# Softmax sums turned on TensorE, evacuating copies given to ScalarE, and 64-column level products, in a four-mixer kernel on one core

## The chip, the cores and the metric

The kernel runs on one core of a Trainium2 chip. The metric is the device time of one execution, in microseconds. A product of two 128-row tiles runs on TensorE (PE), which loads a stationary operand ("weights", the records of PEld) and streams the moving operand past it; VectorE (DVE), ScalarE (ACT) and GpSimd (POOL) do the element-wise work, and every DMA of this kernel is issued by SyncE (SP), in order.

## The reference

x is 1024 tokens by 1024 features in float32. Four mixers follow each other, with normalisations between them:

```python
x = layer_norm(ALPHA * x + gla_mixer(x), ...)        # 4 heads, gated linear attention, chunks of 64
x = layer_norm(ALPHA * x + dilated_mixer(x, k, v))   # 3 groups of windows, 8 query heads, 2 kv heads
for i in (0, 1):
    shift, scale, gate = split(silu(c) @ ada_w[i] + ada_b[i])
    h = rmsnorm(x, g[i]) * (1 + scale) + shift
    x = x + gate * (diff_attention(h) if i == 0 else mla(h))
return rmsnorm(x, final_g)
```

Three places of it matter here. In the gated linear attention, `att[i, j] = sum_d q[i, d] k[j, d] exp(b[i, d] - b[j, d])` for j <= i, with b the running sum of the log gates. In the differential attention each head has two score sets:

```python
p = softmax(sc, axis=-1)
o = (p[:, :, 0] - lam * p[:, :, 1]) @ v          # per head
o = rmsnorm(o, subln_g) * (1 - lambda_init)      # over the head's 128 features
y = (o * silu(z)) @ w_out
```

And the MLA mixer first makes two low-rank projections, normalises them and multiplies them up to heads.

## The kernel before

**Products.** A float32 product is split into three products of fp32r halves (`mm3`, L165 to L167): high by high, high by low, low by high. Weights come by DMA as `wraw` (128x1024) or `wvraw` (128x512), ACT casts them to `whi` or `wvhi` (L192, L204), and `lo` (L150) subtracts to get the low half, on DVE or POOL.

**The order of the work.** PE runs in the order in which the program is written (a manual schedule for PE alone); the other engines' orders, SP's too, are set by the Tile scheduler. Projections are cut into filler units. A `Unit` has a prep (loads and casts) and pieces of some 430 to 655 ns each, and `Fill.give(ns)` puts as many pieces into PE's order as the credit pays for, wherever the main work would leave PE waiting. All filler units, and some of the main work, take their PSUM tile from one pool, "mm", which has two buffers: a piece that begins a third tile waits until the first one has been copied out by its `evac`.

**The stages,** by the profiled execution: gated linear attention to about 395 us (`gla_core`), a boundary (gating, output projection, layer norm) to 520, the preparation of the window attention (gates, V) to 610, its main loop to 1200, a boundary to 1340, the preparation of the differential attention (V, ada) to 1450, its main loop to 2008, a boundary to 2150, the preparation of MLA to 2300, its main loop to 2690, and the final boundary and norm.

**GLA levels** (L465 to L492). Per head, seven levels m = 64, 32, ..., 1. At each one the 1024 positions are pairs of halves of m; `e` holds the decays of earlier halves (L472) and later halves (L473), ACT takes the exponential (L474), DVE multiplies k by it into `ktl` (L476) and q by it in place (L477, 128x1024). Level 64 multiplies `ktl`'s 64 columns by `e`'s 64 (L481). The other six make two PSUM tiles of four 128x128 products each (L489), of which only the later halves' columns are taken by a `copy_predicated` (L490).

**V and gate units.** `u_vs` makes eight units of tokens (st 0 to 7) per group of values; its evac copies 128x256 out of PSUM on ACT for odd st and on DVE for even st (L959 in the window attention, L1285 in the differential attention). `u_gate` (L250) copies a gate's two halves out on ACT (half 0) and DVE (half 1) (L254). MLA's low-rank units copy `lraw` out on DVE (L1485).

**Ada units** (L583 to L589). The prep is eight DVE operations on a 128x4096 weight (one L575, seven L577) that end in `xb`; the piece is one product with `ones` (L583); then DVE masks it, sums it and adds the bias (L586, L588, L589).

**The differential attention's main loop** (L1389 to L1459) runs 66 steps over 8 heads by 8 query tiles. Step i makes the scores of tile i (L1420), their maxima (L1424) and exponentials (L1426), which also give the softmax sums, one column of `dsum` (128x8) for each tile. `combine`, run one step later, joins the two score sets (L1441 to L1443), and after every fourth tile writes four columns of `dsum` to DRAM in token order (L1445):

```python
nc.sync.dma_start(self.dnd[h][:, half(t // 4)].rearrange("o (f p) -> (o p) f", p=128), dsum[:, t - 3:t + 1])
```

Two steps behind the scores, `attend` transposes P (L1240), and copies it out as `PTh` (ACT, L1242) and `PTl` (DVE, L150). After each pair of tiles `pv` multiplies by V (L1365 to L1368), copies the result out as `y` (L1370) and squares it; `norm` sums the squares with a product of ones (L161) and writes them to `d_ms` (L1381). `factors` (L1245) reads the squares (`d_ms`, L1251) and the softmax sums (`d_dn`, L1252) back with tokens on the partitions, works out the reciprocal roots on DVE (L1254 to L1265) and writes them to `d_rs` (L1267). It is called for 14 halves of heads after tile pair (6, 3), for half (7, 0) after (7, 1), and for (7, 1) in the boundary.

Of the kernel before, what the change touches and what calls it, by code (L numbers as in the profile page):

```python
# [11 lines left out]
I32 = mybir.dt.int32  # L12
# [125 lines left out]
class Kern:  # L138
# [124 lines left out]
    def build(self):  # L263
        tc, nc, A = self.tc, self.nc, self.A
        with ExitStack() as ctx:
# [9 lines left out]
            self.ones = cp.tile([128, 128], F32, name="ones")  # L275
            self.ones_r = cp.tile([128, 128], F32R, name="ones_r")
            self.cv = cp.tile([128, 4], F32, name="cv")
# [6 lines left out]
            nc.vector.memset(self.ones_r.bitcast(F32), 1.0)  # L284
# [34 lines left out]
    def gla(self):  # L319
        tc, nc, A = self.tc, self.nc, self.A  # L320
        V, S, G, T = nc.vector, nc.scalar, nc.gpsimd, nc.tensor
        with ExitStack() as ctx:
# [22 lines left out]
            def u_g(h, halves=(0, 1)):  # L345
                return self.u_gate(h, "gla_wg", gp, halves)
# [103 lines left out]
    def gla_core(self, gp, pp, fill, h, qT, kT, v, bs, masks, ahead):  # L450
# [14 lines left out]
        for li, m in enumerate(LEVELS):  # L465
# [11 lines left out]
            V.tensor_tensor(e, qT, e, op=OP.mult)  # L477
            if m == 64:
                pl = pp.tile([128, 8, 64], F32, name="lv")
                for c in range(8):  # L480
                    T.matmul(pl[:64, c, :], kt_[:, c * 128:c * 128 + 64], e[:, c * 128 + 64:c * 128 + 128], start=True, stop=True)  # L481
                V.tensor_copy(att[:64].rearrange("p (c i) -> p c i", i=128)[:, :, 64:128], pl[:64])
                fill.give(2200)
                continue
            for hf in range(2):
                pl = pp.tile([128, 512], F32, name="lv")
                for c in range(4):
                    cc = slice((4 * hf + c) * 128, (4 * hf + c) * 128 + 128)
                    T.matmul(pl[:, c * 128:c * 128 + 128], kt_[:, cc], e[:, cc], start=True, stop=True)  # L489
                V.copy_predicated(view(att[:, half(hf)])[:, :, 1, :],  # L490
                                  masks[:, li * 256:li * 256 + 256].rearrange("p (n m) -> p n m", m=m), view(pl)[:, :, 1, :])
# [189 lines left out]
    def boundary(self, name, wo, res, res_out, warm, ln=None, gate=None, mod=None, normed=False):  # L681
# [151 lines left out]
        for hf, off, n in parts:  # L833
            s = slice(hf * 512 + off, hf * 512 + off + n)
            for kt in range(2 if hf == 0 else 6 if final else 3, 8) if off == 0 else ():
                if normed and hf == 0 and kt == 7:
                    self.factors(bo, [(7, 1)])
# [90 lines left out]
    def swa(self, before):  # L928
# [6 lines left out]
        with ExitStack() as ctx:  # L935
# [13 lines left out]
            with tc.tile_pool(name="swv", bufs=1, reuse_waits="tile") as vp:  # L949
# [235 lines left out]
            def after(h, g):  # L1185
# [13 lines left out]
                if g == 2:  # L1199
                    if h == 2:  # L1200
                        fill.add(u_kk(1, 0))
                    fill.add(self.u_gate(h, "swa_wg", ap, (0, 1) if h > 2 else (1,)))
# [42 lines left out]
    def factors(self, pool, hs):  # L1245

        nc, V = self.nc, self.nc.vector
# [6 lines left out]
        V.scalar_tensor_tensor(e, e, 128.0 * 1e-6, e, op0=OP.mult, op1=OP.mult)  # L1254
        V.tensor_tensor(t, t, e, op=OP.add)
        V.tensor_scalar(t, t, 1.0 / 128.0, None, op0=OP.mult)

        yi = y.bitcast(I32)
        V.tensor_scalar(yi, t.bitcast(I32), 1, None, op0=OP.logical_shift_right)
        V.tensor_scalar(yi, yi, -1.0, float(0x5f3759df), op0=OP.mult, op1=OP.add)  # L1260
        V.tensor_scalar(t, t, -0.5, None, op0=OP.mult)
        for _ in range(4):
            V.tensor_tensor(e, y, y, op=OP.mult)
            V.tensor_tensor(e, e, t, op=OP.mult)
            V.scalar_tensor_tensor(y, e, 1.5, y, op0=OP.add, op1=OP.mult)  # L1265
        for n, (g, hf) in enumerate(hs):
            nc.sync.dma_start(flat(self.rsd[g], hf), y[:, 4 * n:4 * n + 4])  # L1267

    def da(self, before):
# [3 lines left out]
        with ExitStack() as ctx:  # L1273
            with tc.tile_pool(name="dav", bufs=1, reuse_waits="tile") as vp:
# [75 lines left out]
            zs = [self.u_gate(h, "da_wz", dp, (hf,)) for hf, h in [(1, h) for h in range(3)] +  # L1350
# [430 lines left out]
```

## Time and profile before

| | us |
|---|---|
| median of 3 runs | 2798.11 (2795.3 to 2800.18) |
| the profiled execution's own time | 2794.63 |
| its span, first to last instruction | 2792.9 |
| PE busy | 2660.9 (95%) |
| DVE busy | 1890.0 (68%) |
| ACT busy | 1349.2 (48%) |
| POOL busy | 314.6 (11%) |

The profile is of one execution. [...] A wait of PE is idle time of PE with the line of the instruction that waited and the line that ended the wait. The timeline lists single instructions with the idle time before them in brackets. Numbers of lines are those of the kernel before.

### The profile page before, as it was taken

What the parts mean: (1) busy time and instruction counts of PE and PEld (TensorE: products, weight loads), DVE (VectorE), ACT (ScalarE), POOL (GpSimd) and SP (SyncE); (2) the same over time, 40 slices, a digit from 0 to 9 for tenths busy, and PEclk for the clock granted to TensorE, in tenths of its full rate; (3) what the DMA queues carried; (4) which work ended last, traced back from release to release, by engine and by line L of the source; (5) the groups of instructions that cost most, each with busy time, mean ns of one, the idle gap of its engine ahead of it and who ended that gap; (6) DMA issues with size and microseconds to landing.
All of it is one profiled execution on the core that took longest, in us unless ns stands there. A gap on an engine that the chain in (4) does not pass through costs nothing.

```text
span 2792.9 us, 39308 instructions
## 1 busy us (share of the span) xinstructions
PE 2660.9 (95%) x14788; PEld 2234.5 (80%) x14788; DVE 1890.0 (68%) x3478; ACT 1349.2 (48%) x2492; POOL 314.6 (11%) x224
## 2 busy tenths in 40 slices
PE   8999999998999999988999999998799899999998
PEld 7889988887778878776897877786578688888878
DVE  7776547567666666667657788886576627777785
ACT  5444345426344434347515766765445415554563
POOL 0000000000000000000015656664000000000000
PEclk9999999999999999999999999999799999999999
DMA  5310155654111111154642432342275220100143
GB/s 206 107 43 32 49 180 182 210 176 144 50 42 50 46 47 53 50 185 145 228 165 74 63 67 61 66 55 62 90 266 170 68 70 23 33 27 29 39 172 110
DMA packets 163926, 274.70 MB, mean 98 GB/s; under 512 B 32948, under 2 KB 82388, under 8 KB 162072
## 3 DMA queue, kind: packets, MB, share of 16 engines
q1 hardware_dynamic: 163736, 272.19, 31.7%
q8 instruction: 116, 1.90, 0.3%
q14 instruction: 74, 0.61, 0.1%
HBM read 195.48 MB, written 66.17 MB: 94 GB/s over the span
## 4 chain that ended last, share of the span: by engine, by line
PE 67%; DVE 14%; DMA 7%; ACT 7%; issue 3%; SPq 1%; POOL 1%; ACTq 0%; DVEq 0%; POOLq 0%
PE mm L165 14%; PE mm L166 14%; PE mm L167 14%; PE pt L1240 3%; PE sc L1420 3%; PE sc L1657 2%; PE sc L1049 2%; PE lv L489 1%; PE pt L1153 1%; PE sc L166 1%; PE sc L165 1%; PE sc L167 1%; DVE den L1424 1%; PE mm L1623 1%; DVE wlo L150 1%
## 5 line engine op out<-in xcount | busy, mean ns | idle before, releaser
L165 PE MATMUL mm<-xh,whi 128*128 128x512 f32 x1456 | 613.3, 421 | 18.0 <-DVE t L911 6.0
L167 PE MATMUL mm<-xh,wlo 128*128 128x512 f32 x1456 | 574.0, 394 | 2.5 <-POOL wlo L150 1.6
L166 PE MATMUL mm<-xl,whi 128*128 128x512 f32 x1456 | 574.0, 394 | 1.7 <-DVE xl L150 1.7
L165 PEld LDWEIGHTS mm<-xh,whi 128*128 128x128 f32 x1456 | 277.6, 191 | 75.5 <-DVE t L911 7.3
L167 PEld LDWEIGHTS mm<-xh,wlo 128*128 128x128 f32 x1456 | 275.8, 189 | 64.4 <-POOL wlo L150 2.5
L166 PEld LDWEIGHTS mm<-xl,whi 128*128 128x128 f32 x1456 | 277.6, 191 | 52.9 <-DVE xl L150 4.0
L150 POOL TENSOR_TENSOR wlo<-wraw,whi 128x1024 fp32r<-128x1024 f32 x29 | 70.6, 2435 | 1334.9 <-ACT whi L192 1332.9
L165 PE MATMUL mm<-wvhi,xh 128*128 128x256 f32 x704 | 204.6, 291 | 4.8 <-DVE V L959 3.0
L192 ACT CAST whi<-wraw 128x1024 fp32r<-128x1024 f32 (+2 forms) x141 | 135.9, 964 | 138.3 <-PE mm L166 128.9
L167 PE MATMUL mm<-wvhi,xl 128*128 128x256 f32 x704 | 199.2, 283 | 0.1
L166 PE MATMUL mm<-wvlo,xh 128*128 128x256 f32 x704 | 198.6, 282 | 0.0
L1426 ACT ACTIVATE P<-sc,den 128x1024 f32<-128x1024 f32 x128 | 142.9, 1117 | 113.4 <-DVE den L1424 112.8
L1424 DVE TENSOR_REDUCE den<-sc 128x1 f32<-128x1024 f32 x128 | 153.5, 1212 | 3.5 <-PE sc L1420 3.5
L150 DVE TENSOR_TENSOR wlo<-wraw,whi 128x1024 fp32r<-128x1024 f32 (+2 forms) x113 | 123.5, 1093 | 43.8 <-ACT whi L192 40.7
L1043 ACT ACTIVATE P<-P,nm 128x128 f32<-128x128 f32 (+1 forms) x192 | 84.9, 443 | 124.5 <-DVE nm L1041 124.2
L165 PEld LDWEIGHTS mm<-wvhi,xh 128*128 128x128 f32 x704 | 134.0, 190 | 9.9 <-DVE V L959 3.2
L166 PEld LDWEIGHTS mm<-wvlo,xh 128*128 128x128 f32 x704 | 134.5, 191 | 1.3 <-issue 1.0
L167 PEld LDWEIGHTS mm<-wvhi,xl 128*128 128x128 f32 x704 | 133.9, 190 | 0.4 <-DVE xl L150 0.4
L165 PE MATMUL mm<-oh,xh 128*128 128x512 f32 (+1 forms) x336 | 126.1, 375 | 0.3 <-ACT oh L796 0.3
L166 PE MATMUL mm<-ol,xh 128*128 128x512 f32 (+1 forms) x336 | 124.2, 370 | 2.0 <-DVE ol L150 2.0
L167 PE MATMUL mm<-oh,xl 128*128 128x512 f32 (+1 forms) x336 | 123.7, 368 | 0.0
L1053 DVE CUSTOM_DVE_ANT_0 P<-sc,band 128x128 f32<-128x128 f32 (+1 forms) x192 | 59.6, 348 | 71.5 <-PE sc L1049 71.1
(355 smaller groups left out, 6124.5 us busy)
## 6 DMA issues: line engine op xcount, KB each, us to landing
xa<-in_ada_w SPq DMA_DIRECT2D x12, 2048.0 KB
d_z<-zt SPq DMA_DIRECT2D x64, 256.0 KB
oh<-d_z SPq DMA_DIRECT2D x64, 256.0 KB
ol<-d_o SPq DMA_DIRECT2D x64, 256.0 KB
d_r<-X SPq DMA_DIRECT2D x48, 256.0 KB
wraw<-in_swa_wq SPq DMA_DIRECT2D x24, 512.0 KB
res<-d_r SPq DMA_DIRECT2D x40, 256.0 KB
zt<-zt SPq DMA_DIRECT2D x160, 64.0 KB
```

The costliest lines, as they stand in the source:

```text
L150: eng.tensor_tensor(out, src, hi.bitcast(F32), op=OP.subtract)
L165: mm(ps, l[0], r[0], start=first, stop=False)
L166: mm(ps, l[0], r[1], start=False, stop=False)
L167: mm(ps, l[1], r[0], start=False, stop=last)
L192: nc.scalar.copy(hi, raw)
L1043: S.activation(p[:, off:off + w_], p[:, off:off + w_], AF.Exp, bias=nm[:, g, b:b + 1], scale=scale, accum_out=stat(h, g, 1, b))
L1049: T.matmul(sc[:, b % 2, :w_], q[:, b * 128:b * 128 + 128], k[:, k0:k0 + w_], start=True, stop=True)
L1053: V.tensor_tensor_reduce(p[:, off:off + w_], sc[:, b % 2, :w_], mk, 1.0, NEG, op0=OP.add, op1=OP.max, accum_out=stat(h, g, 0, b))
L1240: nc.tensor.transpose(pt[:, i, :], P[:, (4 * j + i) * 128:(4 * j + i) * 128 + 128], self.ident)
L1420: T.matmul(sc[c][:, s], QS[h][c][r, q0:q0 + 128], (KL[h] if k else KH[h][c])[r, s], start=first, stop=not first)
L1424: V.tensor_reduce(dn[:, 2 + c:3 + c], sc[c], AX, OP.max, negate=True)
L1426: S.activation(p, sc[c], AF.Exp, bias=dn[:, 2 + c:3 + c], accum_out=dn[:, 1:2] if c else d0)
```

## The change

It has four parts.

1. **GLA levels.** The query multiplication makes the later halves only: 128x512, into tiles that are named `khT` and `qh` by turns, and no longer in place. The six lower levels' products stream 64 columns in place of 128 (192 products), and a level fills one PSUM tile in place of two. `ones` becomes a view of `ones_r`, which saves one memset.
2. **Softmax sums.** `combine` no longer writes `dsum`. `pv` transposes its four columns on PE (a 4x128 result in unused columns of the PSUM bank that holds its output), ACT copies that out as `dr`, and the write to `d_dn` has 4 rows of 512 bytes. `factors` issues its reads at once, and its DVE work (`rest`) comes two steps later.
3. **Copies.** The copies out of PSUM of the window attention's V, of the differential attention's V, of MLA's `lraw` and of MLA's second gate halves are all made by ACT.
4. **Places of ada units.** In the preparation of the differential attention the first ada product comes three V pieces later and the others at distances of three and four; in MLA's the second one comes after two more gates.

```diff
-    def u_gate(self, h, src, pool, halves=(0, 1), w=None):
+    def u_gate(self, h, src, pool, halves=(0, 1), w=None, act=True):
...
-            (self.nc.vector.tensor_copy if hf else self.nc.scalar.copy)(z, ps)
+            (self.nc.scalar.copy if act or not hf else self.nc.vector.tensor_copy)(z, ps)
...
-            V.tensor_tensor(e, qT, e, op=OP.mult)
+
+            eq = gp.tile([128, 512], F32, name=("khT", "qh")[li % 2])
+            V.tensor_tensor(eq.rearrange("p (n m) -> p n m", m=m), view(qT)[:, :, 1, :], ev[:, :, 1, :], op=OP.mult)
...
+            pl = pp.tile([128, 512], F32, name="lv")
+            for c in range(8):
+                T.matmul(pl[:, c * 64:c * 64 + 64], kt_[:, c * 128:c * 128 + 128], eq[:, c * 64:c * 64 + 64], start=True, stop=True)
             for hf in range(2):
-                pl = pp.tile([128, 512], F32, name="lv")
-                for c in range(4):
-                    cc = slice((4 * hf + c) * 128, (4 * hf + c) * 128 + 128)
-                    T.matmul(pl[:, c * 128:c * 128 + 128], kt_[:, cc], e[:, cc], start=True, stop=True)
...
                 def u_vs(g, sts):
                     def evac(st, ps):
-                        (S.copy if st % 2 else V.tensor_copy)(Vt[g][:, st, :], ps)
+                        S.copy(Vt[g][:, st, :], ps)
...
         for n, (g, hf) in enumerate(hs):
             nc.sync.dma_start(t[:, 4 * n:4 * n + 4], flat(self.msd[g], hf))
             nc.sync.dma_start(e[:, 4 * n:4 * n + 4], flat(self.dnd[g], hf))
-        V.scalar_tensor_tensor(e, e, 128.0 * 1e-6, e, op0=OP.mult, op1=OP.mult)
...
+        def rest():
+            V.scalar_tensor_tensor(e, e, 128.0 * 1e-6, e, op0=OP.mult, op1=OP.mult)
...
+        return rest
...
-                    (S.copy if st % 2 else V.tensor_copy)(t, ps)
+                    S.copy(t, ps)
...
-                    pre.add(u_vs(0, range(4, 8)), u_vs(1, range(4, 5)), ada[0], u_vs(1, range(5, 8)), ada[1], u_vs(2, range(0, 4)), ada[2], u_vs(2, range(4, 8)), ada[3], u_vs(3, range(0, 4)), ada[4], u_vs(3, range(4, 8)), ada[5])
+                    pre.add(u_vs(0, range(4, 8)), u_vs(1, range(4, 8)), ada[0], u_vs(2, range(0, 3)), ada[1], u_vs(2, range(3, 6)), ada[2], u_vs(2, range(6, 8)), u_vs(3, range(0, 1)), ada[3], u_vs(3, range(1, 4)), ada[4], u_vs(3, range(4, 8)), ada[5])
...
-                o = self.mmp.tile([128, 256], F32, name="mm")
+                bank = self.mmp.tile([128, 512], F32, name="mm")
+                o, d = bank[:, :256], bank[0:4, 256:384]
...
+                if due:
+                    T.transpose(d, due[0][2], self.ident)
...
                 nc.sync.dma_start(self.od[h][qb4 // 2][:, s], y)
+                if due:
+                    g, hf, _ = due.pop()
+                    r = dp.tile([128, 128], F32, name="dr")
+                    S.copy(r[0:4], d)
+                    nc.sync.dma_start(self.dnd[g][:, half(hf)].rearrange("o (f p) -> (o f) p", p=128), r[0:4])
...
                 if comb:
                     comb.pop()()
+                if facts and facts[0][0] <= i:
+                    facts.pop()[1]()
...
-                        norm(*nrm)
+                        if f := norm(*nrm):
+                            facts.append((i + 2, f))
...
-                            nc.sync.dma_start(self.dnd[h][:, half(t // 4)].rearrange("o (f p) -> (o p) f", p=128),
-                                              dsum[:, t - 3:t + 1])
+                            due.append((h, t // 4, dsum[:, t - 3:t + 1]))
...
-                        V.tensor_copy(raw[key, hf][:, c, :], ps)
+                        S.copy(raw[key, hf][:, c, :], ps)
...
-                pre.add(self.u_ada(p0, 1, 5, 1), *[self.u_gate(h, "mla_wz", p0) for h in range(3, 8)])
+                late = [self.u_gate(h, "mla_wz", p0) for h in range(3, 8)]
+                pre.add(*late[:2], self.u_ada(p0, 1, 5, 1), *late[2:])
```

The gates of the gated linear attention, of the window attention's main loop and of the differential attention's main loop are called with `act=False` and keep their engines.

How it moves instructions, at three places. **First place:** SP's queue near the end of the differential attention's loop, from the write of the squares of pair (6, 3) to the first reads of half (7, 0). `vr` is `factors`' tile, `d_dn` the softmax sums in DRAM, `d_ms` the squares, `d_rs` the result, `wraw` weights for the boundary. Before:

```order
L179 DMA wraw<-in_w_out 128x1024
L1251 DMA vr<-d_ms 128x4
L1445 DMA d_dn<-dsum 128x4x1
L1371 DMA d_o<-y 128x256
L255 DMA d_z<-zt 128x512
...
L1267 DMA d_rs<-vr 128x4 x14
L1371 DMA d_o<-y 128x256
L1252 DMA vr<-d_dn 128x4
L1381 DMA d_ms<-sq 1x256
L1445 DMA d_dn<-dsum 128x4x1
L1251 DMA vr<-d_ms 128x4
```

With the change:

```order
L1385 DMA d_dn<-dr 4x128
L1254 DMA vr<-d_dn 128x4
L255 DMA d_z<-zt 128x512
L1395 DMA d_ms<-sq 1x256
L179 DMA wraw<-in_w_out 128x1024
L1253 DMA vr<-d_ms 128x4
...
L1271 DMA d_rs<-vr 128x4 x14
L1380 DMA d_o<-y 128x256
L1385 DMA d_dn<-dr 4x128
L1254 DMA vr<-d_dn 128x4
L1395 DMA d_ms<-sq 1x256
L1253 DMA vr<-d_ms 128x4
```

The last read of squares for the 14 halves is no longer followed at once by a write of sums, and the sums of (7, 0) are written after the 14 `d_rs`, directly ahead of their read.

**Second place:** DVE at the same point, around the first instruction of `factors` for the 14 halves (128x56). L1424, with the change L1440, is the maximum of a tile of scores. Before:

```order
L1443 SCALAR_TENSOR_TENSOR P<-P,den 128x1024
L1254 SCALAR_TENSOR_TENSOR vr<-vr 128x56
L150 TENSOR_TENSOR PTl<-pt,PTh 128x4x128
L1424 TENSOR_REDUCE den<-sc 128x1
L150 TENSOR_TENSOR PTl<-pt,PTh 128x4x128
L1424 TENSOR_REDUCE den<-sc 128x1
```

With the change:

```order
L150 TENSOR_TENSOR PTl<-pt,PTh 128x4x128
L1440 TENSOR_REDUCE den<-sc 128x1
L1258 SCALAR_TENSOR_TENSOR vr<-vr 128x56
L1458 RECIPROCAL den<-den 128x1
L1459 SCALAR_TENSOR_TENSOR den<-den,nlam,dsum 128x1
L254 COPY zt<-mm 128x512
L1460 SCALAR_TENSOR_TENSOR P<-P,den 128x1024
```

The first operation of `factors` moves down past six maxima and three combinations (L1443, now L1460). The second one (L1255, now L1259) stays behind the maxima that it followed.

**Third place:** ACT in the preparation of the window attention, where the first four V tiles of the first group are made. L204 casts a piece of V's weights, L741 (now L742) a piece of the normalised x, L959 (now L960) copies a V tile out. Before:

```order
L254 COPY zt<-mm 128x512
L741 CAST xh_70<-X 128x512 x2
L204 CAST wvhi<-wvraw 128x512
L959 COPY V_4095<-mm 128x256
L204 CAST wvhi<-wvraw 128x512
L959 COPY V_4095<-mm 128x256
L755 ACTIVATE rs<-stat 1x512
```

With the change:

```order
L254 COPY zt<-mm 128x512
L742 CAST xh_70<-X 128x512 x2
L960 COPY V_4097<-mm 128x256
L204 CAST wvhi<-wvraw 128x512 x2
L960 COPY V_4097<-mm 128x256 x3
L960 COPY V_4098<-mm 128x256
L756 ACTIVATE rs<-stat 1x512
```

The copy of st 0, which DVE made, stands ahead of both casts, and the copy of st 1, which stood between the two casts, stands behind both.

## Rows read from the trace of the kernel before

**Rows 1.** The page: totals of the engines (name, busy us, share of the span, instructions).

```profile
PE 2660.9 (95%) x14788; PEld 2234.5 (80%) x14788; DVE 1890.0 (68%) x3478; ACT 1349.2 (48%) x2492; POOL 314.6 (11%) x224
```

**Rows 2.** Windows: busy us of PE, PEld, DVE, ACT, POOL; granted clock, DMA share, GB/s.

```profile
1500.00:1900.00 400.00, 398.91 (x2253) 319.34 (x2252) 326.34 (x387) 272.91 (x510) 255.51 (x181) 1.00 0.36 62
1900.00:1950.00 50.00, 40.92 (x206) 31.17 (x205) 33.05 (x42) 28.87 (x53) 20.71 (x15) 0.90 0.20 59
1950.00:2000.00 50.00, 35.67 (x183) 27.37 (x182) 30.38 (x59) 22.82 (x45) 4.46 (x4) 0.81 0.15 38
```

**Rows 3.** Waits of PE: total us, times, longest.

```profile
PE pt L1240 <- DVE PTl L150: 16.2, 4, 6.1
...
PE mm L583 <- DVE xb L577: 7.8, 3, 4.2
...
PE lv L489 <- DVE e L477: 6.4, 6, 1.7
...
PE mm L165 <- DVE lraw L1485: 2.8, 2, 2.4
PE mm L165 <- ACT y L1370: 2.5, 1, 2.5
...
PE mm L165 <- DVE zt L254: 1.7, 1, 1.7
```

**Rows 4.** Timeline of DVE, tail of the differential attention: start, us, instruction, [idle before].

```profile
1928.10 0.22 DVE L1254 SCALAR_TENSOR_TENSOR vr<-vr 128x56 f32<-128x56 f32 x1 [7.03 <-DMA vr<-d_dn]
...
1962.55 0.22 DVE L1255 TENSOR_TENSOR vr<-vr 128x56 f32<-128x56 f32 x1 [9.08 <-DMA vr<-d_ms]
...
1998.66 0.16 DVE L1255 TENSOR_TENSOR vr<-vr 128x4 f32<-128x4 f32 x1 [6.66 <-DMA vr<-d_ms]
```

**Rows 5.** The chain that ended last, same stretch: start, us, what.

```profile
1871.51 1.36 DMA vr<-d_ms
...
1915.26 10.25 DMA d_dn<-dsum
1925.52 2.47 DMA vr<-d_dn
...
1952.72 9.70 DMA vr<-d_ms
```

**Rows 6.** Timeline of SP's queue: issues in the same stretch.

```profile
1953.15 0.43 SPq L1445 DMA_DIRECT2D d_dn<-dsum  x1
...
1974.99 6.49 SPq L1267 DMA_DIRECT2D d_rs<-vr  x14
```

**Rows 7.** Timelines of PE and of its weight loads: bursts of products (records x16, x4).

```profile
73.03 2.02 PE L489 MATMUL lv<-e,ktl 128*128 128x128 f32 x16 [1.08 <-DVE e L477]
...
58.43 1.15 PE L481 MATMUL lv<-e,ktl 128*64 128x64 f32 x16
...
706.11 0.52 PEld L1109 LDWEIGHTS sc<-xb,sel 128*128 128x128 f32 x4 [2.99 <-DVE xb L1100]
...
1699.77 1.04 PE L1240 MATMUL pt<-ident,P 128*128 128x128 f32 x8
```

**Rows 8.** Lines by form: busy us, mean ns.

```profile
L477 DVE TENSOR_TENSOR e<-qT,e 128x1024 f32<-128x1024 f32 x28 | 33.9, 1220 | 0.1
...
L473 DVE TENSOR_TENSOR e<-b 128x512 f32<-128x512 f32 x27 | 18.4, 681 | 0.0
```

**Rows 9.** Timelines of ACT and PE, preparation of the window attention.

```profile
530.16 0.62 ACT L204 CAST wvhi<-wvraw 128x512 fp32r<-128x512 f32 x1 [3.32 <-DMA wvraw<-in_swa_wv]
...
532.75 0.62 ACT L204 CAST wvhi<-wvraw 128x512 fp32r<-128x512 f32 x1 [1.70 <-DMA wvraw<-in_swa_wv]
...
531.10 0.39 PE L165 MATMUL mm<-wvhi,xh 128*128 128x256 f32 x1 [0.52 <-ACT V L959]
```

**Rows 10.** Source line L204, the casts of V's weights: waits, us and times.

```profile
  DMA wvraw<-in_swa_wv: 9.3, 4
```

**Rows 11.** Timeline of PE: an ada product in MLA's preparation.

```profile
2230.67 2.08 PE L583 MATMUL mm<-xb,ones 128*128 128x512 f32 x2 [4.22 <-DVE xb L577]
```

More of the change, by code (lines that the diff above doesn't have):

```diff
@@ L274, in build @@
             self.ident = cp.tile([128, 128], F32, name="ident")
-            self.ones = cp.tile([128, 128], F32, name="ones")
             self.ones_r = cp.tile([128, 128], F32R, name="ones_r")
+            self.ones = self.ones_r.bitcast(F32)
             self.cv = cp.tile([128, 4], F32, name="cv")
@@ L345, in u_g @@
             def u_g(h, halves=(0, 1)):
-                return self.u_gate(h, "gla_wg", gp, halves)
+                return self.u_gate(h, "gla_wg", gp, halves, act=False)
             nc.sync.dma_start(self.vecs, A["vecs"])
@@ L480, in gla_core @@
                 for c in range(8):
-                    T.matmul(pl[:64, c, :], kt_[:, c * 128:c * 128 + 64], e[:, c * 128 + 64:c * 128 + 128], start=True, stop=True)
+                    T.matmul(pl[:64, c, :], kt_[:, c * 128:c * 128 + 64], eq[:, c * 64:c * 64 + 64], start=True, stop=True)
                 V.tensor_copy(att[:64].rearrange("p (c i) -> p c i", i=128)[:, :, 64:128], pl[:64])
@@ L484, in gla_core @@
                 continue
+            pl = pp.tile([128, 512], F32, name="lv")
+            for c in range(8):
+                T.matmul(pl[:, c * 64:c * 64 + 64], kt_[:, c * 128:c * 128 + 128], eq[:, c * 64:c * 64 + 64], start=True, stop=True)
             for hf in range(2):
-                pl = pp.tile([128, 512], F32, name="lv")
-                for c in range(4):
-                    cc = slice((4 * hf + c) * 128, (4 * hf + c) * 128 + 128)
-                    T.matmul(pl[:, c * 128:c * 128 + 128], kt_[:, cc], e[:, cc], start=True, stop=True)
                 V.copy_predicated(view(att[:, half(hf)])[:, :, 1, :],
-                                  masks[:, li * 256:li * 256 + 256].rearrange("p (n m) -> p n m", m=m), view(pl)[:, :, 1, :])
+                                  masks[:, li * 256:li * 256 + 256].rearrange("p (n m) -> p n m", m=m),
+                                  pl[:, hf * 256:hf * 256 + 256].rearrange("p (n m) -> p n m", m=m))
             fill.give(2800)
@@ L836, in boundary @@
                 if normed and hf == 0 and kt == 7:
-                    self.factors(bo, [(7, 1)])
+                    self.factors(bo, [(7, 1)])()
                 gated(hf, kt)
@@ L1201, in after @@
                         fill.add(u_kk(1, 0))
-                    fill.add(self.u_gate(h, "swa_wg", ap, (0, 1) if h > 2 else (1,)))
+                    fill.add(self.u_gate(h, "swa_wg", ap, (0, 1) if h > 2 else (1,), act=False))
             for g in range(3):
@@ L1252, in factors @@
             nc.sync.dma_start(e[:, 4 * n:4 * n + 4], flat(self.dnd[g], hf))
-        V.scalar_tensor_tensor(e, e, 128.0 * 1e-6, e, op0=OP.mult, op1=OP.mult)
[L1255 to L1267, printed above, removed]
+        def rest():
+            V.scalar_tensor_tensor(e, e, 128.0 * 1e-6, e, op0=OP.mult, op1=OP.mult)
+            V.tensor_tensor(t, t, e, op=OP.add)
+            V.tensor_scalar(t, t, 1.0 / 128.0, None, op0=OP.mult)
+            yi = y.bitcast(I32)
+            V.tensor_scalar(yi, t.bitcast(I32), 1, None, op0=OP.logical_shift_right)
+            V.tensor_scalar(yi, yi, -1.0, float(0x5f3759df), op0=OP.mult, op1=OP.add)
+            V.tensor_scalar(t, t, -0.5, None, op0=OP.mult)
+            for _ in range(4):
+                V.tensor_tensor(e, y, y, op=OP.mult)
+                V.tensor_tensor(e, e, t, op=OP.mult)
+                V.scalar_tensor_tensor(y, e, 1.5, y, op0=OP.add, op1=OP.mult)
+            for n, (g, hf) in enumerate(hs):
+                nc.sync.dma_start(flat(self.rsd[g], hf), y[:, 4 * n:4 * n + 4])
+        return rest
     def da(self, before):
@@ L1349, in da @@
             fill = Fill()
-            zs = [self.u_gate(h, "da_wz", dp, (hf,)) for hf, h in [(1, h) for h in range(3)] +
+            zs = [self.u_gate(h, "da_wz", dp, (hf,), act=False) for hf, h in [(1, h) for h in range(3)] +
                   [(hf, h) for h in range(3, 8) for hf in range(2)]]
@@ L1382, in norm @@
                 if (h, qb4) in FACT:
-                    self.factors(dp, FACT[h, qb4])
+                    return self.factors(dp, FACT[h, qb4])
             FACT = {(6, 3): [(h, hf) for h in range(7) for hf in range(2)], (7, 1): [(7, 0)]}
-            nrm, comb = None, []
+            nrm, comb, due, facts = None, [], [], []
             for i in range(64 + 2):
```

1 line of the change is left out of this document (removed).

## The prediction

> **What bounds the kernel now.** I read the page first. PE is busy in 95% of the span [rows 1], so a step is worth something only where PE waits, or where PE's own work shrinks. The windows come next: from 1500 to 1900 us PE is busy in 398.9 of 400 us, and nothing off PE can gain there. The next two windows of 50 us, the end of the differential attention's loop, hold only 40.9 and 35.7 us [rows 2]. Their granted clock is 0.90 and 0.81: at two levels, 1.00 and 0.50, that is half speed in 20% and 38% of the time, together 29 us. With PE busy in 77% of it, some 22 us of busy time would take 11 at full speed. So 76.6 us busy are some 65.5 us of full-speed work, and these 100 us hold about 34 that are lost. The waits of PE by line [rows 3] tell what else to price: 16.2 us on `PTl` (that same tail), 7.8 on `xb` of the ada units, 6.4 on L477, and smaller ones on copies out of PSUM.
>
> Who holds the tail? DVE does not run there for lack of work but stands still three times, 7.03, 9.08 and 6.66 us, each time in `factors` for a read of `d_dn` or `d_ms` [rows 4]; the `PTl` that PE wants stands behind it on DVE. The chain names the transfers: a write of `dsum` takes 10.25 us to land and its read back 2.47; a read of `d_ms` takes 9.70, where an earlier one took 1.36 [rows 5]. The slow read was issued at 1952.72 and another `dsum` write 0.43 us later [rows 6]: 512 elements of 4 bytes beside it. PE's full clock breaks down after each of the rests.
>
> **The change part by part.**
>
> *Softmax sums, the tail.* 16 writes of 512 separate elements become 16 writes of 4 rows. No row shows a write of 4 rows of 512 bytes; its nearest rows are the reads, 1.36 and 2.47 us [rows 5], and at the far end is the old write, 10.25. I take 2.5, since it has fewer pieces than either. Then the sums of the 14 halves lie ready when DVE comes to its first operation, which besides stands six maxima further down, and the 7.03 us go to zero. The read of `d_ms` no longer has a slow write beside it: 9.08 us become 1 to 2 (2.5 us from issue, less what DVE still has ahead). For half (7, 0) the new write stands behind 14 `d_rs` issues of 6.49 us in all [rows 6], with its read directly behind it; but the operation on it also moves down two steps, so 6.66 us become 0 to 3. DVE's stops fall by 19 to 22 of 22.8 us. PE also loses its one wait of 2.5 us on `y` [rows 3], which ACT made late because SP held the loads of the rope tiles behind a read of `d_dn`. And without the rests some of the 11 us of half clock come back: I count 4, because after 1962 us no filler units are left, PE follows DVE's chain of combination, `PTl` and maximum, and short rests go on. That makes 19 + 2 + 4 = **25 us**; the bounds are 16 (PE's own rests on `PTl`, 16.2, and nothing more) and 31 (nearly all of the 34).
>
> [...] No run here shows the new size yet.
>
> *Softmax sums, the loop.* 16 transposes are added on PE, where it has no slack. Eight transposes of 128x128 take 1.04 us [rows 7], 0.13 each: **+2 us**, bounds 1 and 4 (a 4-column weight could load faster; a bank held longer could cost as much again). 16 copies of 4x128 on ACT, some 0.3 us each, lie beside PE: ACT is busy in 273 of 400 us [rows 2], and its copy of `y` stands ahead of them. If that cover went, they would cost 5.
>
> *GLA.* DVE saves half of L477: 1.22 us for 1024 columns against 0.68 for 512 [rows 8], 0.54 in each of 28, 15 us in all; but PE waits on it only six times, 6.4 us in sum [rows 3], and each of those waits shrinks by up to 0.54 or by what it was, and the products need one tile less to be free. That gives 3 to 5. The products themselves: sixteen records at L489 take 2.02 us, 0.126 each, with 128 weight columns and 128 streamed. L481, 64 and 64, takes 1.15, or 0.072. Which of the two operands sets the pace? L1109 has 128 weight columns and 32 or 64 streamed ones, and four of its loads take 0.52, or 0.13 each [rows 7]. So the weights set it, and 128 weight columns remain. I take **-5 us** in all; bounds -1 and -26 (the pace of L481, in a rival).
>
> *Preparation of the window attention.* This goes against the change. PE's fourth V tile starts at 531.10, as soon as ACT has copied the second one out; that copy stood between two casts which wait for DMAs and start at 530.16 and 532.75 [rows 9]. PE resumed 0.94 us after the start of the first cast. Now the copy stands behind both, and 0.94 after the second is 533.7, 2.6 us later: **+2.6 us**, bounds 0 (the loads come sooner) and 5 (the same again at the second group). The first tile's copy, now ahead of both casts, is early enough.
>
> *Preparation of the differential attention.* Of the 7.8 us on `xb` [rows 3], 4.2 are MLA's [rows 11]; 3.6 belong here. Ada products move apart to three or four V tiles, and DVE sheds 8 of 16 copies. **-2.5 us**, bounds 0 and -3.6, as ACT's copies can be late in the same way as above.
>
> *Preparation of MLA.* Three copies of DVE's that PE waited for go to ACT: `lraw` 2.8 and `zt` 1.7 us [rows 3]. ACT has casts ahead of `lraw` that end late, so I give 0.8 of the first and all of the second. The second ada product waits 4.22 us and then runs at half clock, 2.08 us for what takes half of that otherwise [rows 11]; two gates, some 21 us of PE's work, come ahead of it now. That is 4.2 + 1.3. **-8 us**, bounds -4 and -11.
>
> *Sum.* -25 + 2 - 5 + 2.6 - 2.5 - 8 = **-36 us**, with ends of -12 (16, 4, 1, 5, 0 and 4 in that order) and, the rival of the narrow products apart, about -51. The profiled execution took 2794.6, which gives 2758.6. It lies 3.5 us under the median of the three runs; to the median I therefore predict 2798 - 36 = **2762 us**.
>
> **The rivals.**
>
> *A, the narrow products pay on PE.* If a product of 128 weight columns and 64 streamed ones went at L481's pace, 384 records would each save 0.126 - 0.072 = 0.054 us, 21 us, and the time would be about 2741. For it: PE is busy in that stage, so each ns would count. Against it: the L1109 loads. [...]
>
> *B, the tail keeps its stops.* If the read of `d_ms` is slow for a reason other than the write beside it (the 512 KB of weights issued just ahead, the pieces of 16 bytes of the read itself), the 9.08 us stay; and (7, 0)'s chain of 14 issues, write and read keeps the 6.66. Then only 7.03 + 2.5 of the tail goes, and with 1 us of clock 10 in place of 25: 2777. For it: the read has the same small pieces as before. Against it: an earlier one took 1.36 us.
>
> *C, ACT becomes the one that holds PE, slower.* ACT takes its queue in order, and casts of V's weights wait in it for DMAs. 28 such casts (12 in the window attention's preparation, 16 in the differential attention's) could each hold a copy out of PSUM as the one above is held, for 2.6 us: up to 73. It decides from 14 held ones on, where the 36 us are used up; with 17 the time is about 2806. For it: all V copies now stand in that queue. Against it: in the window attention's preparation, where they waited longest, only four of the casts waited for a DMA at all, 9.3 us in sum [rows 10].
>
> *D, the change is made but the small write stays slow.* If 4 rows of 512 bytes take the 10 us of before, the stop of 7.03 us still goes, as the operation moves down, but the queue of SP stays stuck in the loop and (7, 0) gets worse by its write: about 2780, inside B's case.
>
> **How the numbers follow.** A measurement of this kernel can tell 0.2%, 5.6 us, from no change. I give the forecast 0.63, A 0.09, B with D 0.18, C 0.05, and 0.05 to mixed mishaps that use up the gain within 0.2%. Forecast, A and B are all faster by more than 0.2%, 0.90 together; I take 0.01 off for B joined to the bad ends of the others: 0.89 faster, 0.06 the same, 0.05 slower. The range takes in A on its low side and B with half of the bad ends on its high side: 2741 to 2785.
>
> **What would show it.** In the profile after: no row of DVE with 7 us on `d_dn`, a `d_ms` read of under 3 us, PE busy over 85 of the 100 us that end the loop; L477's form 128x512 at 0.68, the bursts at L489's successor still about 2 us (A: about 1.2); a wait of PE on an ACT copy that ends near 533.7 us; no 4 us wait on `xb` in MLA. The prediction is wrong if DVE's stops in the tail stay over 10 us in sum, or if PE's waits on ACT's V copies exceed 10.

## The result and the profile after

The changed kernel takes 2768.84 us (median of 4 runs, 2768.02 to 2770.05) against 2799.14 before: a ratio of 0.9894, 95% interval 0.9877 to 0.9911, or 30 us. The profiled execution's span is 2765.9 us against 2792.9, 27 us shorter.

The windows of the changed kernel over the differential attention's loop and its tail, with the columns of [rows 2]:

```profile
1500.00:1890.00 390.00, 387.07 (x2195) 309.87 (x2193) 318.77 (x377) 267.72 (x511) 249.30 (x176) 1.00 0.21 61
...
1900.00:1950.00 50.00, 49.73 (x283) 39.71 (x282) 40.36 (x51) 34.26 (x64) 24.25 (x15) 1.00 0.25 72
1950.00:1985.00 35.00, 29.68 (x182) 23.82 (x182) 30.87 (x69) 20.91 (x44) 2.81 (x3) 0.95 0.16 42
```

The tail holds 79.4 us of PE in 85, at a granted clock of 1.00 and 0.95 (the profile's share of full speed). DVE's timeline there, the answer to [rows 4]:

```profile
1941.53 0.22 DVE L1258 SCALAR_TENSOR_TENSOR vr<-vr 128x56 f32<-128x56 f32 x1
...
1951.61 0.22 DVE L1259 TENSOR_TENSOR vr<-vr 128x56 f32<-128x56 f32 x1 [2.85 <-DMA vr<-d_ms]
...
1977.45 0.17 DVE L1258 SCALAR_TENSOR_TENSOR vr<-vr 128x4 f32<-128x4 f32 x1 [0.40 <-DMA vr<-d_dn]
1978.50 0.16 DVE L1259 TENSOR_TENSOR vr<-vr 128x4 f32<-128x4 f32 x1 [0.44 <-DMA vr<-d_ms]
```

DVE's three stops, 22.8 us together, have become 3.7 (2.85, 0.40 and 0.44). SP's queue shows the new write of the 14 halves' last sums; the read behind it waits for the write (4.5 us in two waits from 1930 to 1985 us, the longest 2.6):

```profile
1937.46 0.28 SPq L1385 DMA_DIRECT2D d_dn<-dr  x1
1939.65 0.32 SPq L1254 DMA_DIRECT2D vr<-d_dn  x1
...
1948.00 0.38 SPq L1253 DMA_DIRECT2D vr<-d_ms  x1
```

That is at most 2.2 us from issue to landing, where the old write took 10.25 [rows 5] (at most 3.4 for the write of half (7, 0), behind the 14 `d_rs`); and the read of `d_ms` lands in 3.6 (1948.00 to 1951.61), where it took 9.70.

The waits of PE after the change, to be read beside [rows 3]:

```profile
PE mm L165 <- ACT zt L254: 5.0, 3, 4.2
PE mm L584 <- DVE xb L578: 4.1, 1, 4.1
...
PE o L531 <- DVE st L535: 3.4, 1, 3.4
...
PE mm L165 <- ACT lraw L1501: 3.3, 2, 3.1
PE ms L548 <- DVE sq L546: 3.1, 1, 3.1
PE mm L165 <- ACT vs L1290: 2.9, 2, 2.6
PE mm L167 <- DVE wlo L150: 2.5, 2, 2.3
...
PE pt L1241 <- DVE PTl L150: 1.3, 2, 1.1
```

`PTl` has fallen from 16.2 to 1.3, and the waits on L477 and on `y` are gone; but six of the waits shown are new or grown, and four of them name ACT's copies or the state `st` of the linear attention. To see what each stage gave, I took one event at each border from the profiles (first or last record of a line, by its start) and the lengths between them:

| us | before | changed |
|---|---|---|
| start to the first product with V of GLA's first head | 101.9 | 97.5 |
| start to the last sum of squares of GLA | 386.4 | 387.5 |
| from there to the first window score | 248.5 | 250.2 |
| last window score to first differential score | 306.0 | 308.4 |
| first to 25th copy of `y` in the loop | 374.8 | 377.1 |
| 25th to last copy of `y` (the tail) | 124.3 | 96.4 |
| last `y` to the first score of MLA | 301.3 | 294.1 |

The tail gives 28 us and the boundary with MLA's preparation 7; the other stages give nothing or pay. Each length is of one execution; how far it spreads is told below.

### The profile page after: what moved, and what is told of

It is laid out like the page before. It is cut to its first block, busy times and chain, and to the rows that moved or that the text cites. A ratio compares the mean times of both kernels' runs of the same rounds, so it can differ in the third digit from the quotient of the medians.

```text
span 2765.9 us, 39351 instructions
## 1 busy us (share of the span) xinstructions
PE 2653.7 (96%) x14804; PEld 2232.6 (81%) x14804; DVE 1858.8 (67%) x3431; ACT 1368.3 (49%) x2554; POOL 313.0 (11%) x224
## 4 chain that ended last, share of the span: by engine, by line
PE 69%; DVE 14%; ACT 6%; DMA 6%; issue 3%; SPq 1%; POOL 0%; ACTq 0%; DVEq 0%; POOLq 0%
PE mm L165 15%; PE mm L166 15%; PE mm L167 15%; PE pt L1241 3%; PE sc L1436 3%; PE sc L1674 2%; PE sc L1050 2%; PE lv L488 1%; DVE den L1440 1%; PE pt L1154 1%; DVE P L1460 1%; DVE wlo L150 1%; PE mm L1640 1%; PE mm L1637 1%; PE mm L1638 1%
## 5 line engine op out<-in xcount | busy, mean ns | idle before, releaser
L1440 DVE TENSOR_REDUCE den<-sc 128x1 f32<-128x1024 f32 x128 | 153.0, 1211 | 0.3 <-PE sc L1436 0.2
```

Of the source, the lines that this page charges most:

```text
L1440: V.tensor_reduce(dn[:, 2 + c:3 + c], sc[c], AX, OP.max, negate=True)
```

## The experiments

Twelve runs were made, two of them repeats. One program's executions lie several us apart (the kernel before from 2789.7 to 2803.6 us in one comparison), so effects of a few us are read from the stage lengths of several profiles, and the times beside them with their intervals.

**The softmax sums alone.** The kernel before with part 2 of the change (and the merged `ones`).

> The kernel before with the softmax-sum part alone (transposed sums, contiguous write, later arithmetic of factors). My theory: all of the change's gain in the differential attention's loop comes from here and from nothing else: the tail loses its three stops, -28 us, and the loop pays about +2.5 for 16 transposes: -25 us, about 2774. Rival: part of that tail's gain came from work that the other parts had moved (the loop began 5 us later in the changed kernel): then -15 to -20.

Measured: 2773.35 us, ratio 0.9922 (0.9904 to 0.9939), 22 us. Its tail is 95.7 us long, its loop to the 25th copy 377.5. The time lies between my theory and the rival, and its interval (17 to 27 us) holds some of each; the lengths decide: with nothing else changed the tail is as short as in the changed kernel. So the tail's gain and the loop's price come from this part alone.

**Which half of it?** The two edits below are given against the kernel of the softmax sums alone, and each shows its main lines. First the turned write with the arithmetic at once (`factors` runs to its end in one call):

```diff
...
-                    return self.factors(dp, FACT[h, qb4])
+                    self.factors(dp, FACT[h, qb4])
...
```

> The kernel before with the sums turned on TensorE and written in 4 rows, but with the arithmetic of factors called at once as before. My theory: the small write is the whole of the tail's gain; VectorE's order shows the first operation of factors six maxima further down already through the later write, so the two-step delay adds nothing: -20 to -25 us against before, as with the whole softmax-sum part. Rival: the delay is what keeps VectorE from standing still, and without it one or two of the stops (7 and 9 us) come back: -5 to -12 us.

Measured: 2774.09 us, ratio 0.9924 (0.9911 to 0.9936); tail 97.9 us. Then the delay with the old write (no transpose, no copy `dr`):

```diff
...
-                            due.append((h, t // 4, dsum[:, t - 3:t + 1]))
+                            nc.sync.dma_start(self.dnd[h][:, half(t // 4)].rearrange("o (f p) -> (o p) f", p=128),
+                                              dsum[:, t - 3:t + 1])
```

> The kernel before with the arithmetic of factors called two steps later, but with the sums written element by element as before. My theory: VectorE's order has the first operation at its old place, and the read of the squares still has the slow write beside it, so the stops of 7, 9 and 7 us stay: within 4 us of before. Rival (the delay does it): -10 to -20 us.

Measured: 2795.48 us, ratio 1.0 (0.9989 to 1.0012); tail 125.1 us. DVE's stops with the delay and the old write:

```profile
1932.33 0.22 DVE L1256 SCALAR_TENSOR_TENSOR vr<-vr 128x56 f32<-128x56 f32 x1 [6.72 <-DMA vr<-d_dn]
...
1963.38 0.70 DVE L1257 TENSOR_TENSOR vr<-vr 128x56 f32<-128x56 f32 x1 [5.47 <-DMA vr<-d_ms]
...
1998.91 0.16 DVE L1257 TENSOR_TENSOR vr<-vr 128x4 f32<-128x4 f32 x1 [5.55 <-DMA vr<-d_ms]
```

and with the turned write and no delay:

```profile
1935.57 0.21 DVE L1253 SCALAR_TENSOR_TENSOR vr<-vr 128x56 f32<-128x56 f32 x1
...
1945.70 0.22 DVE L1254 TENSOR_TENSOR vr<-vr 128x56 f32<-128x56 f32 x1 [2.88 <-DMA vr<-d_ms]
...
1973.68 0.16 DVE L1254 TENSOR_TENSOR vr<-vr 128x4 f32<-128x4 f32 x1 [0.29 <-DMA vr<-d_ms]
```

The stops with the delay alone are 17.7 us in sum, 5 fewer than before, and yet nothing of the time is gained. The turned write is all of it that can be told: its tail of 97.9 us lies among those of the nine profiles with write and delay (95.5 to 99.1). The same pair shows that the read of `d_ms` is slow for the write beside it and not for its own small pieces, since the read is the same in both. SP's queue with the old write,

```profile
1957.17 0.37 SPq L1251 DMA_DIRECT2D vr<-d_ms  x1
1957.59 0.43 SPq L1451 DMA_DIRECT2D d_dn<-dsum  x1
```

and with the turned one:

```profile
1942.06 0.38 SPq L1250 DMA_DIRECT2D vr<-d_ms  x1
```

From issue to DVE's start the read takes 9.8 us before, 6.2 with the delay, and 3.6 with the turned write; for half (7, 0) it is 8.8, 8.0 and 1.8. The turned write is smaller in pieces and also stands elsewhere in the queue, and no run separates the two. The weights issued just ahead of the longer read (rival B) are in all of them; the 3.6 us against 1.8 may be theirs, which no run shows.

**The levels alone.** The kernel before with part 1.

> The kernel before with the level part alone (later halves' queries, 64 streamed columns). My theory: TensorE's pace is set by the 128 weight columns, so the bursts stay at about 2 us per 16 records, and the 6.4 us of waits on the query product that go are taken back at the next fixed point, the state of the second head behind the gate chain, which ScalarE holds up by its wait for the output weights (wo): between -2 and +3 us against before, about 2800. Rival (the forecast's): the 6.4 us are kept, -5 us. Rival (narrow products pay): -20 us.

Measured: 2790.86 us, ratio 0.9985 (0.9974 to 0.9996), 1 to 7 us; the profile's last sum of squares comes at 385.7 us against 386.4. The interval holds the forecast's 5 us and touches my theory (at most 2 us faster) at its end, so it doesn't decide between them; the -20 of the narrow products is out. The products show the same: here is the form of the changed kernel's products, and one burst of sixteen,

```profile
L488 PE MATMUL lv<-khT,ktl 128*128 128x64 f32 x192 | 22.7, 271 | 0.0
```

```profile
85.97 1.89 PE L488 MATMUL lv<-khT,ktl 128*128 128x64 f32 x16
```

The burst of before in [rows 7] took 2.02, but it came after a wait; one without a wait took

```profile
62.48 1.95 PE L489 MATMUL lv<-e,ktl 128*128 128x128 f32 x16
```

Half the streamed columns, at the same 128 weight columns, save 0.06 to 0.13 us of a burst; with 64 weight columns and 64 streamed sixteen records took 1.15 [rows 7]. What became of the waits is in the timelines of the changed kernel, ACT first, then PE:

```profile
92.34 1.06 ACT L613 ACTIVATE wo<-wo 128x1024 f32<-128x1024 f32 x1 [7.83 <-DMA wo<-in_gla_wo]
...
100.84 1.06 ACT L613 ACTIVATE wo<-wo 128x1024 f32<-128x1024 f32 x1 [3.27 <-DMA wo<-in_gla_wo]
101.90 0.67 ACT L440 ACTIVATE ab<-lv,vecs 128x512 f32<-128x512 f32 x1
```

```profile
110.48 0.80 PE L531 MATMUL o<-qh,st 128*128 128x128 f32 x2 [3.39 <-DVE st L535]
```

PE comes 4.4 us earlier to the first products with V. But ACT stands in its queue for the loads of the output weights (`wo`, one buffer: load, centre, store, load), with the second half of the next head's gate chain (L440) behind it; DVE waits 2.80 us for that chain ahead of its scan (107.42 to 110.0), and the state `st` that PE wants stands behind the scan, at 109.97. PE loses 3.4 us there and 3.1 at the sum of squares after it (1.5 before), and the clock in these windows is 0.91 and 0.85, where before it is 1.00 in both:

```profile
100.00:120.00 20.00, 16.61 (x77) 13.74 (x76) 12.52 (x22) 12.91 (x16) 0.00 (x0) 0.91 0.22 82
120.00:140.00 20.00, 16.90 (x86) 14.13 (x85) 9.40 (x15) 10.25 (x13) 0.00 (x0) 0.85 0.23 79
```

Is it ACT's wait for `wo`? The test leaves the centring of the first mixer's output weights out:

```diff
-            nc.scalar.activation(raw[0], raw[0], AF.Copy, accum_out=m)
-            nc.vector.tensor_scalar(m, m, -1.0 / 1024.0, None, op0=OP.mult)
-            nc.vector.tensor_scalar(raw[0], raw[0], m, None, op0=OP.add)
+            if i:
...
```

> The changed kernel without the centring of the first mixer's output weights: they are loaded and stored as they are, ScalarE's sum over them and VectorE's subtraction are left out. My theory: ScalarE's waits for these loads, ahead of the second head's gate chain in its queue, took back what the levels gained; without them TensorE's 3.4 us wait on the state and its half clock after it go, and the first mixer ends 4 to 8 us earlier than in the changed kernel (at about 380 to 383 us for its last sum of squares, 387.5 now): 2761 to 2765. Rival: the gate chain is bound by VectorE and ScalarE themselves, and nothing moves by over 2 us.

Measured: the last sum of squares at 382.1 us, against 387.5 and, in the repeat, 386.0; the wait on `st` is not there any more. The same two windows in its profile, to be read beside those above, and PE's wait at the sum of squares:

```profile
100.00:120.00 20.00, 20.00 (x103) 16.68 (x102) 13.32 (x23) 11.47 (x14) 0.00 (x0) 1.00 0.16 59
120.00:140.00 20.00, 16.90 (x100) 15.04 (x99) 10.03 (x16) 8.35 (x10) 0.00 (x0) 0.83 0.21 75
```

```profile
129.38 2.07 PE L548 MATMUL ms<-sq,ones_r 128*128 128x512 f32 x2 [3.10 <-DVE sq L546]
```

The 4 to 5 us were there, and the centring took them: from the first product with V to the last sum of squares it takes 284.5 to 284.7 us in the six profiles with the old levels, 288.6 to 290.3 in the seven with the new ones, and 284.9 here. The variant takes away ACT's waits for `wo` and the passes over it as well (1.06 us each on ACT, 0.75 on DVE); that the waits are the larger part is read from the timeline, and no run leaves the centring out with the old levels. The clock is another matter. The wait of 3.10 us at the sum of squares and the low clock behind it stay without the centring (0.83 in the second window; the two products at 129.38 take 2.07 us, those at 113.31 1.02), and in the repeat of the changed kernel the products behind the same 3.40 us on `st` are not slower (0.39 us for the two L529 at 110.52, 0.63 here at 111.07); why the sum of squares is waited for longer with the new levels stays open.

The variant's total, 2765.34 us (0.9892, 0.9878 to 0.9906), isn't apart from the changed kernel's: by its profile the first differential score comes at 1475.5 us, against 1480.3 and 1478.3, and the last instruction at 2764.0, against 2765.9 and 2764.5, so most of the gain is given back later. Across the profiles the same shows: with the new levels and the centring the last sum of squares comes at 385.7 to 388.2 us (seven profiles), with the old levels at 384.9 to 387.3 (six): earlier at the first product, and no earlier at the end.

**The copies and the ada places alone.** Parts 3 and 4.

> The kernel before with the copies on ScalarE and the ada units' new places alone. My theory: -7 in MLA's preparation, +3 in the differential attention's preparation, +1 to +3 in the window attention's: -1 to -4 us, about 2796. Rival (the forecast's terms: -8, -2.5, +2.6): -8 us, about 2791.

Measured: 2793.22 us, ratio 0.9994 (0.9981 to 1.0007); in the profile 294.7 us from the last `y` to MLA's first score, 306.2 for the differential preparation, 250.0 to the first window score. The time is nearer my theory, and the 8 us of the forecast are outside the interval. (The profile is of the fastest of twelve executions, 7 us under their median.)

**The two V stages taken back,** together, then one by one.

```diff
-                        S.copy(Vt[g][:, st, :], ps)
+                        (S.copy if st % 2 else V.tensor_copy)(Vt[g][:, st, :], ps)
...
-                    S.copy(t, ps)
+                    (S.copy if st % 2 else V.tensor_copy)(t, ps)
```

(and, in the differential attention, the old line of ada places.)

> The changed kernel with both V stages as before: even tiles copied by VectorE again in the window and the differential attention's preparations, ada products of the latter at their old places; levels, softmax sums and MLA's part stay. My theory: ScalarE's queue (casts that wait for DMAs, copies that wait for stores) cost the changed kernel there: 3 to 6 us faster than the changed kernel, about 2764. Rival (the forecast's): these copies gain 0 net, so within 1 us of it, or slower by 2.5 us as the waits on the ada operand come back.

> The changed kernel with the even V tiles of the window attention copied by VectorE again. My theory: ScalarE's queue in that preparation costs 2 to 4 us, seen in the start of the main loop's scores (637.7 us now, 634 to 636 then): about 2766. Rival (the wait is on the gate's copy, which stays on ScalarE): under 1 us.

> The changed kernel with the differential attention's preparation as before (even V tiles copied by VectorE, ada units at their old places). From the last score of the window attention to the first of the differential one it took 306.1 us before and 308.4 in the changed kernel. My theory: ScalarE's queue (waits for stores of V and for casts) and the ada operand cost that; 305 to 306.5 here, and 2 to 3 us off the changed kernel's time. Rival (the forecast's -2.5): the old places cost more, 309 or over.

Measured: 2765.14 us (0.9891, 0.9872 to 0.991) for both, 2772.72 (0.992, 0.9907 to 0.9932) for the window attention's alone, 2770.61 (0.991, 0.9895 to 0.9924) for the differential's. The stages: from the last sum of squares to the first window score 246.5 and 246.4 us where its V copies are taken back, 252.6 where they aren't (250.2 in the changed kernel); for the differential preparation 305.2 and 305.3 us where they are taken back, 309.8 where not (308.4). In the window attention the changed kernel has

```profile
527.89 0.58 PE L165 MATMUL mm<-wvhi,xh 128*128 128x256 f32 x1 [4.23 <-ACT zt L254]
```

```profile
520.00:540.00 20.00, 15.57 (x107) 15.04 (x106) 14.16 (x22) 11.41 (x21) 0.00 (x0) 0.83 0.72 221
```

and with the window attention's copies taken back

```profile
527.41 0.38 PE L165 MATMUL mm<-wvhi,xh 128*128 128x256 f32 x1 [2.97 <-DVE V L960]
```

```profile
520.00:540.00 20.00, 16.82 (x131) 15.87 (x130) 16.05 (x26) 11.55 (x20) 0.00 (x0) 1.00 0.71 227
```

A wait of 3 us on DVE's copy has become one of 4.2 on ACT's gate copy. In the changed kernel windows of 1 us show a clock of 0.50 from 527 to 533 us, and the products behind the longer wait take 0.41 us up to 532.97 and 0.28 from 533.36; in the repeat, too, they take 0.41 behind its 4.23 us. Behind the 2.96 us of the kernel before, and the 2.97 here and with both V stages taken back, they take 0.28. The length of the wait alone doesn't decide on the clock: the 3.39 and 3.40 us on `st` above differ in what follows. Nor does the loss show with the old levels: there the stage takes 250.0 us with all copies on ACT and 248.5 to 250.2 in five profiles with half of them on DVE. In the differential preparation the changed kernel has, on ACT and on PE,

```profile
1380.85 0.73 ACT L1290 COPY vs<-mm 128x256 f32<-128x256 f32 x2 [3.89 <-DMA d_v<-vs]
```

```profile
1381.27 0.38 PE L165 MATMUL mm<-wvhi,xh 128*128 128x256 f32 x1 [2.61 <-ACT vs L1290]
...
1403.78 2.04 PE L584 MATMUL mm<-xb,ones_r 128*128 128x512 f32 x2 [4.14 <-DVE xb L578]
```

ACT waits 3.89 us for a store of V to give a buffer back, PE 2.61 for ACT, and the ada wait has only moved. In all five profiles with the new copies and places these two waits of PE come to 4.5 to 7.7 us, against 2.9 to 3.8 at the ada products of the nine others; copies and places changed together, and no run separates them. Yet the single stages' gains don't reach the time: both one-by-one kernels are slower than the changed one by their medians.

**The repeats.** The changed kernel once more, and the kernel with both V stages taken back once more.

> The changed kernel once more, beside its variants on one chip: -28 to -31 us against before. No theory differs on it; its profile is to show which of its waits return from one execution to the next (the 3.4 us on the state near 110 us, the 4.2 us on the gate's copy near 528 us, the 4.1 us on the ada operand near 1404 us).

> The changed kernel with both V stages as before, once more beside the changed kernel on one chip. My theory: 3 to 5 us faster than it. Rival: equal within 1.5 us, the difference of the single profiles being the clock of the tail.

Measured on one chip: 2766.71 us (0.9898, 0.9881 to 0.9916) and 2766.52 (0.9898, 0.9881 to 0.9915). The rival holds: there is no difference that these runs can tell. The changed kernel's repeat shows the 3.40 us on `st` and the 4.23 on the gate's copy again, and in the differential preparation 3.05 on `vs` and 2.5 on the ada operand. The other kernel's two profiles are 2762.3 and 2770.1 us long: the same program took 305.2 us in one and 308.0 in the other for the differential preparation, and 298.1 and 301.5 from the last `y` to MLA's first score. So with the new levels the window attention's loss is found in every profile (250.0 to 252.6 us in four with its copies on ACT, 246.4 to 248.0 in four without), but the gain from taking it back is not kept to the end.

**Without levels and V copies.**

> The kernel before with the softmax sums and MLA's copies and ada place alone, without the levels and without the V copies. My theory: levels are worth 0 to 2 us once the state's wait takes them back, so this is within 3 us of the kernel without V copies (no_v_copies) and at -28 to -31 us against before. Rival: the levels carry 5 us, and it is 5 us slower than that one.

Measured: 2764.86 us (0.9889, 0.9872 to 0.9906), with levels 2766.52: nothing between them that these runs can tell. Nor can they tell it from the changed kernel, though it has fewer edits.

## Why the prediction was right

The sum was -36 us, measured -30, inside the range, and the forecast case came. By the two profiles' stages the terms are -28, +2, +1, +2, +2 and -7, in the order of the sum: the tail, two thirds of the forecast, carried it, and two of the three smaller gains did not come. Its steps one by one:

- **The tail** (-25): right in the mechanism. 124.3 to 96.4 us, 28 us; stops of 22.8 us are 3.7. The write of 4 rows takes at most 2.2 us (taken 2.5), and the slow read of `d_ms` was the neighbour's doing, shown by the turned write alone; it still takes 3.6, not under 3. The split was off: PE's waits on `PTl` and `y` that went are 18.7 us (taken 21), and the clock gave back some 10 in place of 4. That is an estimate from windows of 2.5 us: PE's busy time at half clock (0.50) cost 12 us of the tail before and under 2 after. So the 3 us over are two errors that partly cancel. That the first operation moves down is an effect of the later write, not of the delay: with the delay alone it stays and the time doesn't move. Rival D is out, and of B at most the 2 us are left that the read takes longer than that of (7, 0).
- **The loop** (+2, bounds 1 and 4): mis-sized. 374.8 to 377.1 us, and 377.1 to 377.7 in all ten profiles with the transposes against 373.8 to 374.8 in the four without. By the 25th copy twelve of the sixteen are done; the means are 2.95 us apart, so by that estimate one costs 0.25 us with all that comes with it, not 0.13, and sixteen some 4. The copy `dr` takes 0.25 us and PE does not wait for it.
- **GLA** (-5): the pace was right (1.89 us a burst, rival A is out), the kept gain was wrong. The step that failed is "each of those waits shrinks by up to 0.54 or by what it was": the waits did go, but I didn't ask what is late next. It was the gate chain of the second head behind ACT's wait for `wo`; without the centring the 4 to 5 us are there. By the times alone the levels are worth between 1 and 7 us without the other parts, and nothing that shows beside them.
- **The window attention** (+2.6): right in sign, wrong in place. No wait of PE ends near 533.7 us; it came 6 us earlier, as 4.2 us on the gate's copy. ACT's copy of the second V tile did come late (534.94), and that PE did not wait for it is put down to its clock (0.50 from 527 to 533 us), which is argued and not tested. The stage lost 1.6 us against before, and 3.2 to 3.8 against the same kernel with its copies on DVE.
- **The differential preparation** (-2.5): wrong in sign. 308.4 us against 306.0. What failed is "Ada products move apart ... and DVE sheds 8 of 16 copies": ACT's copies wait for a store of V (3.89 us), and the ada wait only moved, from 3.6 us at 1381 and 1392 to 4.1 at 1404 (2.5 in the repeat). With one program spread over 305.2 to 308.0 the size of this loss stays open.
- **MLA** (-8): mis-sized. From the first `lraw` copy to MLA's first score it takes 160.9 to 165.3 us in the nine profiles with this part and 164.3 to 167.3 in the five without; the means, 163.4 and 166.3, are 3 us apart. The ada and gate part held: from the last `lraw` copy to the score 106.2 to 107.9 against 112.7 to 114.2, with no wait on `xb` of 4 us left (of the 1.3 us for its clock, the row shows only 1.04: 2.08 us for two products that take 1.02 with the change). `lraw` itself got worse, from the first copy to the last 54.6 to 57.4 against 51.5 to 53.1, because on ACT it stands behind casts, those of `ck` (1.28 us for two at 2152.44, the copy at 2154.48). The prediction named such casts, but priced the move as a gain of 0.8:

```profile
2155.12 0.79 PE L165 MATMUL mm<-xh,whi 128*128 128x512 f32 x1 [3.09 <-ACT lraw L1501]
...
2200.68 0.50 PE L167 MATMUL mm<-xh,wlo 128*128 128x512 f32 x1 [2.29 <-DVE wlo L150]
```

So the tail carried the change, and the small gains of the rest were largely lost, mostly behind something in ACT's queue: rival C's mechanism, at a small part of its price (PE's waits on ACT's V copies are 2.9 us). Why the other variants with the softmax sums and MLA's part need 297.9 to 301.5 us from the last `y` to MLA's first score, where the changed kernel needs 294.1 and 294.7, isn't settled, and no run takes it apart.

## What to carry to other kernels

Look for the transfer that stands beside a slow one: here the read issued just ahead of a write of 512 elements of 4 bytes took 9.70 us in the profile before, and 3.6 with the write in 4 rows, and with the change DVE's stops in the tail went from 22.8 us to 3.7 and PE's waits on `PTl` from 16.2 to 1.3. When a wait on the path goes, follow PE to the next operand whose time is set by something that has not moved (here a load in ACT's queue, which it waited 7.83 us for), and price the gain only up to there. Moving a copy from one engine's queue to another's moves what it waits behind (here 3.89 us for a store of V on ACT); list that engine's loads, stores and casts ahead of it first.

## What the runs showed of the hardware

Products with 128 weight columns and 64 streamed ones took 1.89 us per 16 records, with 128 streamed 1.95 to 2.02. A write of 512 separate elements took 10.25 us to land, one of the same 2 KB in 4 rows at most 2.2; and a read that took 6.2 to 9.7 us beside the first takes 3.6 without it. A loop with twelve transposes of a 128x4 tile on PE, with their copies and writes, is 2.95 us longer, an estimate of 0.25 each, where a 128x128 transpose in a run of eight takes 0.13. And rests of PE of one length were not followed by the same pace each time: after the 3.39 and 3.40 us at 110 in two profiles of one program, two L529 products took 0.63 us (the clock from 110 to 112 is 0.51) and 0.39; after 2.97 us in the preparation of the window attention the 128x256 products took 0.28 us, and after 2.94 in that of the differential attention (without levels and V copies) they took 0.41 from 1381.07 to 1384.06.
